# Up projection by Strassen's seven products, groups of 264 tokens, and a down stage that reads its input back from DRAM

## The chip, the cores and the metric

One core of one Trainium2 chip runs the whole kernel. The metric is the device time of one execution, in microseconds. The kernel before takes 1574.02 us (median of three runs, 1573.68 to 1574.51).

## What is computed

One layer over 1024 prompt tokens and 8 samples of 4 tokens (1056 tokens in all, 1024 features): a norm, a mixer (three kinds of recurrent heads between the products with `w_in` and `w_out`), a residual, and then the ConvFFN between two norms, with a second residual:

```
x  = x + rms_norm(mix, norm_mix_post)
hn = rms_norm(x, norm_ffn_pre)                      # x * rsqrt(mean(x * x)) * weight
up = einsum('bld,df->blf', hn, w_up)                # 1024 -> 2 * 2816
gate, val = up[..., :D_FF], up[..., D_FF:]
gate = causal_dwconv(gate, state, w, b)             # three taps along the tokens
out  = einsum('blf,fd->bld', gelu(gate) * val, w_down)   # 2816 -> 1024
x  = x + rms_norm(out, norm_ffn_post)
```

## The kernel before

Features lie on the 128 partitions, tokens along the row. The 1056 tokens are cut into `NG = 3` groups of `G = 352`. Every dense product works on a tile of 128 output features: `load_w` (L256 to L267) fetches a weight tile, ACT rounds it to `wh` (L264), POOL subtracts to get the remainder `wl` (L265), and the moving operand is held in the same way as `hh` and `hl`. `dense` (L269 to L278) then does three matmuls for each 128 features of the contraction: wh with hh, wh with hl, wl with hh. They are recorded under L203. Such a matmul has 352 columns.

The program is a sequence of parts:

- Mixer. The products with `w_in` fill the gaps of the recurrent chains; the order of the tensor engine is made by `Weave`, which places a step of a chain when a table `WAIT` of estimated times (ns) says its operands are there.
- Output projection, `project`, five tiles of `w_out` at first and the rest group by group; when a group has its sums of squares, `finish(g)` is woven in. It computes the norm's factor (`rstd_of`: a product with ones into a tile `po`, then Ln and Exp on ACT), and for each 128 features multiplies it in (L1629), adds the residual (L1630), writes the result to `x1_dram`, and splits it into `hh[g]` and `hl[g]` (`split_scaled`, L333) without waiting for the second norm. After `WAIT["f_rows"]` the factor of the second norm, `rs`, is made. From the end of this part on the tensor engine's order is no longer written by hand.
- ConvFFN. It goes through the 22 tiles of hidden features in five `QUARTERS`. For a tile, `gate_conv` multiplies a gate tile with all three groups (24 matmuls each), `scaled` (L303) multiplies the accumulated sums by `rs` on DVE on their way from PSUM to `fpre`, ACT does one tap (L212), DVE the other two (L1682), and ACT the gelu. `value` does the same product for the value tile, DVE multiplies (L303, L1695), ACT rounds to `hidh` (L1700), DVE subtracts to `hidl` (L1701). Both stay in SBUF until the down products of that quarter: 8 output tiles by 3 groups, added into `fa` by DVE (L1734).
- The last quarter's down products go group by group, so that the final norm and the output of a group run beside the products of the next.

In all the tensor engine does 7704 of these 352-column matmuls: 2376 with `w_in`, 576 with `w_out`, 3168 up, 1584 down. The lines below carry the up stage:

```
w = load_w(I["w_up"][2 * f], KD)                              # one 512 KB transfer, one cast, one subtraction
ps = drain(dense(accp, w, hn_operand, KD, g))                 # 24 matmuls
scaled(pre[:, 2 + g * G:2 + (g + 1) * G], ps, g, 0, G)
...
nc.scalar.copy(out=hidh[:, groups[g]], in_=hid)
vtt(out=hidl[:, groups[g]], in0=hid, in1=hidh[:, groups[g]].bitcast(F32), op=ALU.subtract)
```

Of the kernel before, what the change touches and what calls it, by code (L numbers as in the profile page):

```python
# [8 lines left out]
F32 = mybir.dt.float32  # L9
# [11 lines left out]
DS = 4  # L21
# [3 lines left out]
G = 352  # L25
NG = 3
# [5 lines left out]
QUARTERS = ((0, 5), (5, 10), (10, 14), (14, 18), (18, 22))  # L32
# [3 lines left out]
# (kind, unit, tiles as (section, tile in the section, conv tile or None))  # L36
# [6 lines left out]
# the order of the dense work of the mixer  # L43
# [3 lines left out]
# columns of the packed vectors  # L47
# [22 lines left out]
CUT = 4  # L70
# [23 lines left out]
def constants():  # L94
# [5 lines left out]
    # what takes the place of NEG and LV for the samples  # L100
# [92 lines left out]
def kernel(ctx: ExitStack, tc: tile.TileContext, I, O):  # L193
# [31 lines left out]
    hnp = ctx.enter_context(tc.tile_pool(name="hnp", bufs=1))  # L225
    wp = ctx.enter_context(tc.tile_pool(name="wp", bufs=2))
    left, right = ExitStack(), ExitStack()
# [22 lines left out]
    x1_dram = drp.tile([NG, P, KD, G], F32, name="x1_dram")  # L250
# [32 lines left out]
    def hn_operand(k, g):  # L283
        return hh[g][:, k, :], hl[g][:, k, :]
# [1596 lines left out]
```

## Time and profile before

| | |
|---|---|
| median of three runs | 1574.02 us |
| span of the profiled execution | 1578.6 us |
| busy: PE, DVE, ACT, POOL | 95%, 58%, 34%, 35% |
| mean granted clock of PE | 0.977 |
| bytes moved | 100.63 MB, 64 GB/s |

The profiled execution is 4.6 us above the median of the runs. A matmul's record stands for the time from its issue to its modelled end, so records overlap; the distance from one start to the next is what a matmul costs in a stream. PEld is the loading of weights, which runs beside PE. POOL is GpSimd, SP the engine that issues the transfers (its queue is SPq), and its instructions go out in order. In the records a granted clock of 1 is 2.4 GHz on the tensor engine, and stretches at half of that are 1.2 GHz.

### The profile page before, as it was taken

How to read it: one execution, taken by the hardware profiler on the slowest of the kernel's cores; microseconds unless marked ns; L12 is line 12 of the kernel's file. 1: busy time of each engine (PE TensorE's matmuls, PEld its weight loads, DVE VectorE, ACT ScalarE, POOL GpSimd, SP SyncE). 2: the span in 40 equal slices, each digit the busy share in tenths (PEclk: the TensorE clock that was granted, in tenths of full speed). 3: DMA queues.
4: the chain of work that ended last, by engine and by line, in shares of the span. 5: the costliest groups of instructions: out<-in, count | busy, mean ns of one | idle time of the engine just before them, and what ended most of it. 6: DMA issues, size and time to landing. Idle time of an engine off the chain costs nothing.

```text
span 1578.6 us, 24157 instructions
## 1 busy us (share of the span) xinstructions
PE 1496.2 (95%) x9438; PEld 1453.1 (92%) x9438; DVE 920.7 (58%) x1818; ACT 542.1 (34%) x1173; POOL 546.1 (35%) x624
## 2 busy tenths in 40 slices
PE   8788999989999999999899999999999999999995
PEld 8788899879989989988889999999999999999994
DVE  6889888796474367636975522444245325424558
ACT  7644445443342232424652211221122112212353
POOL 6234433232354353566432122221222222122224
PEclk9989999999999999999999999999999999999997
DMA  5111010111111231324531112111111111111142
GB/s 180 43 48 30 23 45 25 34 32 30 43 55 47 79 112 47 102 76 152 187 100 41 44 42 62 41 41 42 52 54 34 41 61 42 40 55 54 52 151 110
DMA packets 51210, 100.63 MB, mean 64 GB/s; under 512 B 14857, under 2 KB 25737, under 8 KB 50713
## 3 DMA queue, kind: packets, MB, share of 16 engines
q1 hardware_dynamic: 51096, 99.10, 20.1%
q8 instruction: 74, 1.21, 0.3%
q14 instruction: 40, 0.32, 0.1%
HBM read 85.25 MB, written 13.31 MB: 62 GB/s over the span
## 4 chain that ended last, share of the span: by engine, by line
PE 63%; DVE 17%; ACT 6%; POOL 5%; issue 4%; DMA 4%; SPq 0%; DVEq 0%; POOLq 0%; ACTq 0%
PE acc L203 55%; PE mc L203 3%; PE mb L203 3%; DVE kq L465 2%; PE mb L207 2%; DMA E<-rows_dram 2%; POOL wl L265 1%; DVE hl L333 1%; DVE two L784 1%; DVE v L465 1%; ACT sq L212 1%; POOL E L868 1%; PE po L203 1%; DVE fs L344 1%; ACT E L212 1%
## 5 line engine op out<-in xcount | busy, mean ns | idle before, releaser
L203 PE MATMUL acc<-hh,wh 128*128 128x352 f32 x1952 | 660.7, 339 | 18.2 <-DVE pre L303 12.2
L203 PE MATMUL acc<-hh,wl 128*128 128x352 f32 x1960 | 635.8, 324 | 2.6 <-POOL wl L265 2.0
L203 PE MATMUL acc<-hl,wh 128*128 128x352 f32 x1952 | 631.9, 324 | 0.7 <-DVE hl L333 0.7
L203 PEld LDWEIGHTS acc<-hh,wh 128*128 128x128 f32 x1952 | 371.7, 191 | 25.3 <-DVE pre L303 8.5
L265 POOL TENSOR_TENSOR wl<-w,wh 128x1024 fp32r<-128x1024 f32 (+2 forms) x117 | 252.9, 2162 | 362.3 <-ACT wh L264 354.8
L203 PEld LDWEIGHTS acc<-hh,wl 128*128 128x128 f32 x1960 | 372.4, 190 | 4.2 <-POOL wl L265 2.3
L203 PEld LDWEIGHTS acc<-hl,wh 128*128 128x128 f32 x1952 | 373.0, 191 | 3.1 <-DVE hl L333 1.7
L264 ACT CAST wh<-w 128x1024 fp32r<-128x1024 f32 (+2 forms) x117 | 109.9, 939 | 416.4 <-PE acc L203 400.3
L203 PE MATMUL acc<-hidh,wh 128*128 128x352 f32 x444 | 143.8, 324 | 0.0
L203 PE MATMUL acc<-hidh,wl 128*128 128x352 f32 x444 | 143.3, 323 | 0.0
L203 PE MATMUL acc<-hidl,wh 128*128 128x352 f32 x444 | 143.2, 322 | 0.0
L303 DVE TENSOR_TENSOR fpre<-acc,rs 128x352 f32<-128x352 f32 (+1 forms) x88 | 35.8, 430 | 137.5 <-PE acc L203 135.1
L1734 DVE TENSOR_TENSOR fa<-fa,acc 128x352 f32<-128x352 f32 x96 | 49.8, 519 | 106.3 <-PE acc L203 105.9
L1682 DVE SCALAR_TENSOR_TENSOR fy<-fpre,vec,fy 128x1072 f32<-128x1072 f32 x44 | 79.3, 1802 | 36.7 <-ACT fy L212 36.0
L203 PEld LDWEIGHTS acc<-hidh,wh 128*128 128x128 f32 x444 | 83.4, 188 | 0.0
L203 PEld LDWEIGHTS acc<-hidl,wh 128*128 128x128 f32 x444 | 83.4, 188 | 0.0
L203 PEld LDWEIGHTS acc<-hidh,wl 128*128 128x128 f32 x444 | 83.4, 188 | 0.0
L1701 DVE TENSOR_TENSOR hidl<-hid,hidh 128x352 fp32r<-128x352 f32 x66 | 52.7, 799 | 37.8 <-ACT hidh L1700 37.8
L1677 POOL COPY ffn_o<-fpre 128x2 f32<-128x2 f32 x22 | 4.1, 186 | 157.8 <-DVE fpre L303 157.8
L465 DVE SCALAR_TENSOR_TENSOR kq<-pre,cw,kq 128x352 f32<-128x352 f32 (+1 forms) x72 | 53.4, 748 | 7.7 <-ACT kq L212 7.2
L1700 ACT CAST hidh<-hid 128x352 fp32r<-128x352 f32 x66 | 31.9, 483 | 74.2 <-DVE hid L1695 49.9
L303 DVE TENSOR_TENSOR hid<-acc,rs 128x352 f32<-128x352 f32 x66 | 34.4, 521 | 38.1 <-PE acc L203 38.1
(552 smaller groups left out, 2238.7 us busy)
## 6 DMA issues: line engine op xcount, KB each, us to landing
w<-in_w_up_dram SPq DMA_DIRECT2D x44, 512.0 KB
w<-in_w_in_dram SPq DMA_DIRECT2D x30, 512.0 KB
E<-rows_dram SPq DMA_DIRECT2D x24, 256.0 KB
w<-in_w_dn_dram SPq DMA_DIRECT2D x21, 256.0 KB
w<-in_w_out_dram SPq DMA_DIRECT2D x10, 512.0 KB
w<-in_w_dn_dram SPq DMA_DIRECT2D x16, 320.0 KB
xr<-in_xT_dram SPq DMA_DIRECT2D x24, 176.0 KB
hh<-x_dram SPq DMA_DIRECT2D x3, 1408.0 KB
```

The source lines that it names most:

```text
L203: return nc.tensor.matmul(out, **kw)
L207: return nc.tensor.transpose(out, in_, identity)
L212: i = nc.scalar.activation(**kw)
L264: nc.scalar.copy(out=wh[:, ks], in_=w[:, ks])
L265: gtt(out=wl[:, ks], in0=w[:, ks], in1=wh[:, ks].bitcast(F32), op=ALU.subtract)
L303: vtt(out=out, in0=ps, in1=r, op=ALU.mult)
L333: stt(out=hl[g][:, k, :], in0=x, scalar=col(vcol + k), in1=hh[g][:, k, :].bitcast(F32), op0=ALU.mult, op1=ALU.subtract)
L465: stt(out=y[:, a:b], in0=pre[:, a + j:b + j], scalar=cw2[:, 4 * t + j:4 * t + j + 1], in1=y[:, a:b], op0=ALU.mult, op1=ALU.add)
L1682: stt(out=y[:, :LF], in0=pre[:, j:j + LF], scalar=col(V_FW + 3 * f + j), in1=y[:, :LF], op0=ALU.mult, op1=ALU.add)
L1700: nc.scalar.copy(out=hidh[:, groups[g]], in_=hid)
L1701: vtt(out=hidl[:, groups[g]], in0=hid, in1=hidh[:, groups[g]].bitcast(F32), op=ALU.subtract)
L1734: vtt(out=fa[:, g, m, :], in0=fa[:, g, m, :], in1=ps[:, :G], op=ALU.add)
```

## The change

The groups become four of 264 tokens everywhere, so all dense products now have 264 columns: 3168 matmuls with `w_in`, 768 with `w_out`, 2112 down.

The up product is made for pairs of output tiles, two halves of the contraction and pairs of token groups, that is as a 2 by 2 by 2 block product, with seven products instead of eight (Strassen's scheme in Winograd's form). `fast` does one pair of tiles for one or both pairs of groups (a unit `u`): seven products of 12 matmuls each, 168 matmuls for both units. Gate and value make 22 such calls, 3696 matmuls in all. The pair number 0 of the gate is made in two calls, one for each unit, with its weight pieces made twice.

`weight_pieces` fetches four pieces of 256 KB in a call, adds and subtracts them on DVE (four instructions of 128x512), and `weight_piece` rounds each of the seven to a high part on ACT and a remainder on POOL. `operands` makes the seven combinations of tokens once, in `finish`, on DVE and POOL (instructions of 128x1056), after the tokens were multiplied by the factor of the second norm (eight more instructions per group, L1649). `scaled` is gone from the FFN. The sums of products are put together on DVE as they come out of PSUM (`f6`, `f7`, `out`).

What the value side makes, `hid`, is written to `hid_dram` (22 transfers of 528 KB), read back in a down stage that begins after all up products (`hx`), and rounded and split there (ACT, DVE, 128x1056). The quarters are six. The tensor engine's order is written by hand to the end. The estimates in `WAIT` and the places of the norms of the input (`RSTD`) have other values.

```
-G = 352
-NG = 3
+G = 264
+NG = 4
-QUARTERS = ((0, 5), (5, 10), (10, 14), (14, 18), (18, 22))
+QUARTERS = ((0, 2), (2, 6), (6, 10), (10, 14), (14, 18), (18, 22))
-    s_norm=6310, rows1=9000, rows2=6960, rows3=8500, f_rows=18400, f_0=5120, f_1=8920,
+    s_norm=6310, rows1=9000, rows2=6960, rows3=8500, f_rows=14000, f_0=4000, f_1=5000, f_2=8000, f_last=3000,
-RSTD = [(1, 1), (1, 6), (2, 4)]
+RSTD = [(1, 1), (2, 1), (3, 1), (3, 6)]
+    hid_dram = drp.tile([NF, P, T], F32, name="hid_dram")
 def finish(g, wait=0):
...
-                split_scaled(m, k, V_FPRE, g)
                 square_sum(on, m, s2, k)
             yield WAIT["f_rows"]
-            if g == 1:
+            if g == NG - 2:
                 yield lambda: "projected" in have
-            rstd_of(new_rs(g), s2[:1])
+            r = rstd_of(on.tile([P, G], F32, name="rstd"), s2[:1])
+            for k in range(KD):
+                m = mix[k][:, groups[g]]
+                stt(out=m, in0=m, scalar=col(V_FPRE + k), in1=r, op0=ALU.mult, op1=ALU.mult)
+            operands(*divmod(g, 2))
+            have.add(("normed", g))
+        def operands(u, q):
...
+            t1, t2 = (on.tile([P, KH, G], F32, name=f"xt{i}") for i in range(2))
+            vtt(out=t1, in0=B[0][1], in1=B[0][0], op=ALU.subtract)
+            vtt(out=t2, in0=B[1][1], in1=t1, op=ALU.subtract)
+            split(6, t2)
+            split(5, t1, True)
+            vtt(out=B[0][1], in0=B[1][1], in1=B[0][1], op=ALU.subtract)
+            split(7, B[0][1])
+            gtt(out=t2, in0=B[1][0], in1=t2, op=ALU.subtract)
+            split(4, t2, True)
+            split(3, B[1][1])
+    QS = [(1, 0, 1), (6, 1, 0), (5, 2, 0), (7, 1, 0), (2, 0, 0), (4, 1, 0), (3, 2, 0)]
+        def weight_piece(x):
...
+            nc.scalar.copy(out=wh, in_=x)
+            gtt(out=wl, in0=x, in1=wh.bitcast(F32), op=ALU.subtract)
+        def weight_pieces(srcs):
...
+            for i, j in ((0, 0), (1, 0), (1, 1), (0, 1)):
+                A[i][j] = w[:, KH * i:KH * i + KH] if j == 0 else fg.tile([P, KH, P], F32, name="wq", bufs=2)
+                dma(out=A[i][j], in_=srcs[i][:, KH * j:KH * j + KH])
+            s1, s2 = (fg.tile([P, KH, P], F32, name=f"ws{i}") for i in range(2))
+            yield weight_piece(A[0][0])
+            vtt(out=s1, in0=A[1][0], in1=A[1][1], op=ALU.add)
+            vtt(out=s2, in0=s1, in1=A[0][0], op=ALU.subtract)
+            yield weight_piece(s2)
+            yield weight_piece(s1)
+            vtt(out=A[1][0], in0=A[0][0], in1=A[1][0], op=ALU.subtract)
+            yield weight_piece(A[1][0])
+            yield weight_piece(A[0][1])
+            yield weight_piece(A[1][1])
+            vtt(out=s2, in0=A[0][1], in1=s2, op=ALU.subtract)
+            yield weight_piece(s2)
+        def fast(srcs, units, out):
+            for (p, b, _), (wh, wl) in zip(QS, weight_pieces(srcs)):
+                for u in units:
...
+                    for k in range(KH):
+                        mm(ps, lhsT=wh[:, k, :], rhs=xh[:, k, :], start=first and k == 0, stop=False, **kw)
+                        mm(ps, lhsT=wh[:, k, :], rhs=xl[:, k, :], start=False, stop=False, **kw)
+                        mm(ps, lhsT=wl[:, k, :], rhs=xh[:, k, :], start=False, stop=k == KH - 1, **kw)
+                    if p == 1:
+                        nc.scalar.copy(out=sb[u, 1], in_=ps)
+                    elif p in (6, 7):
+                        vtt(out=sb[u, p], in0=sb[u, 1], in1=ps, op=ALU.add)
...
+                for j in range(2):
+                    dma(out=hid_dram[2 * i + j], in_=hids[j])
...
+            for f in range(f0, f1):
+                x = fp.tile([P, T], F32, name="hx", bufs=2)
+                dma(out=x, in_=hid_dram[f])
+                h, l = (fp.tile([P, T], F32R, name=f"hid{y}{f - f0}", bufs=2) for y in "hl")
+                nc.scalar.copy(out=h, in_=x)
+                vtt(out=l, in0=x, in1=h.bitcast(F32), op=ALU.subtract)
```

Three places of the order show what is moved. The first is DVE where the norms of the last token group end and the up products begin (`hl2`, `s20`, `mv` belong to `finish`, `fpre` to the gate; `ws` and `w` are weight pieces). Before:

```order
L333 SCALAR_TENSOR_TENSOR hl2_8179<-mkq_898,vec_75,hh2_8178 128x352 [waits Activation_49]
L1629 SCALAR_TENSOR_TENSOR mv_899<-mv_899,vec_75,rstd_8171 128x352
L341 TENSOR_TENSOR s20_8176<-s20_8176,s21_8177 128x352 [waits DVE_49,PE_49,Pool_49]
L1630 TENSOR_TENSOR mv_899<-mv_899,xr_8246 128x352 [waits DMAHW4_49,DVE_49]
L333 SCALAR_TENSOR_TENSOR hl2_8179<-mv_899,vec_75,hh2_8178 128x352 [waits Activation_49]
L344 TENSOR_TENSOR s20_8176<-s20_8176,sq1_8253 128x352 [waits Activation_49]
L303 TENSOR_TENSOR fpre_8288<-acc_8291,rs0_8079 128x352 [waits DMAHW5_49,DMAHW3_49,DMAHW6_49,DMAHW1_49,DMAHW7_49,DMAHW0_49,PE_49]
L303 TENSOR_TENSOR fpre_8288<-acc_8317,rs1_8166 128x352
```

After, at the same place, for the third of the four groups:

```order
L1649 SCALAR_TENSOR_TENSOR mix_1107<-mix_1107,vec_75,rstd_9571 128x264 [waits DMAHW6_49]
L1649 SCALAR_TENSOR_TENSOR mix_1107<-mix_1107,vec_75,rstd_9571 128x264 [waits DMAHW0_49]
L1649 SCALAR_TENSOR_TENSOR mix_1107<-mix_1107,vec_75,rstd_9571 128x264 [waits DMAHW3_49]
L1649 SCALAR_TENSOR_TENSOR mix_1107<-mix_1107,vec_75,rstd_9571 128x264 [waits DMAHW5_49]
L1649 SCALAR_TENSOR_TENSOR mix_1107<-mix_1107,vec_75,rstd_9571 128x264 [waits DMAHW7_49]
L1662 TENSOR_TENSOR hl6_9585<-mix_1107,hh6_9584 128x1056 [waits PE_49,Activation_49]
L1720 TENSOR_TENSOR ws1_9600<-ws0_9599,w_9592 128x512
L1723 TENSOR_TENSOR w_9592<-w_9592 128x512
L1727 TENSOR_TENSOR ws1_9600<-wq_9597,ws1_9600 128x512 [waits DMAHW2_49,Pool_49]
```

Before, the last DVE instructions of `finish` are followed by sums that leave PSUM, and no weight passes through DVE. After, the second weight piece that the first up product needs from DVE (`ws1_9600`) stands behind the eight norm multiplications of the group and a subtraction of 128x1056.

The second place is DVE in the middle of the up stage, before:

```order
L303 TENSOR_TENSOR fpre_8577<-acc_8632,rs2_8257 128x320 [waits PE_49]
L303 TENSOR_TENSOR fpre_8577<-acc_8632,rs2_8257 128x8x4
L1682 SCALAR_TENSOR_TENSOR fy_8661<-fpre_8577,vec_75,fy_8661 128x1072 [waits Activation_49]
L1682 SCALAR_TENSOR_TENSOR fy_8661<-fpre_8577,vec_75,fy_8661 128x1072 [waits DVE_49]
L303 TENSOR_TENSOR hid_8699<-acc_8674,rs0_8079 128x352 [waits PE_49]
L1695 TENSOR_TENSOR hid_8699<-fy_8467,hid_8699 128x352 [waits DVE_49]
L1701 TENSOR_TENSOR hidl1_8667<-hid_8699,hidh1_8666 128x352 [waits Activation_49]
L303 TENSOR_TENSOR hid_8729<-acc_8704,rs1_8166 128x352 [waits PE_49]
```

and after, from the end of a gate pair (L1784) into its value pair:

```order
L1784 TENSOR_TENSOR fpre_10732<-f6_10809,accr_10826 128x8x4
L1800 SCALAR_TENSOR_TENSOR fy_10967<-fpre_10732,vec_75,fy_10967 128x1072 [waits Activation_49]
L1800 SCALAR_TENSOR_TENSOR fy_10976<-fpre_10733,vec_75,fy_10976 128x1072 [waits Activation_49]
L1800 SCALAR_TENSOR_TENSOR fy_10967<-fpre_10732,vec_75,fy_10967 128x1072 [waits DVE_49]
L1800 SCALAR_TENSOR_TENSOR fy_10976<-fpre_10733,vec_75,fy_10976 128x1072 [waits DVE_49]
L1754 TENSOR_TENSOR f6_11043<-f1_11009,accr_11030 128x264 [waits PE_49,Activation_49]
L1754 TENSOR_TENSOR f6_11058<-f1_11024,accr_11045 128x264 [waits PE_49,Activation_49]
L1719 TENSOR_TENSOR ws0_11237<-w_11230,wq_11233 128x512 [waits DMAHW5_49,DMAHW4_49,Pool_49]
L1723 TENSOR_TENSOR w_11230<-w_11230 128x512 [waits DMAHW3_49,DVE_49,Pool_49]
L1754 TENSOR_TENSOR f7_11105<-f1_11009,accr_11030 128x264 [waits PE_49]
```

Before, the two taps (L1682) of one tile stand between sums of whole tiles. After, four taps (L1800) stand in a row ahead of `f6`, and the weight sums of the next call (L1719, L1723) stand ahead of `f7`, whose read of PSUM must be over before the sixth product of the same call adds to that bank.

The third is SP at the first down products, before:

```order
L263 DMA w_8959<-in_w_up_dram 128x1024 [waits DMAHW5_49,Pool_49]
L263 DMA w_9056<-in_w_up_dram 128x1024 [waits DMAHW6_49,Pool_49]
L263 DMA w_9155<-in_w_up_dram 128x1024 [waits DMAHW7_49,Pool_49]
L263 DMA w_9253<-in_w_dn_dram 128x640 [waits DMAHW1_49,DMAHW0_49,Pool_49]
L263 DMA w_9310<-in_w_dn_dram 128x640 [waits DMAHW1_49,Pool_49]
L263 DMA w_9367<-in_w_dn_dram 128x640 [waits DMAHW2_49,Pool_49]
```

and after:

```order
L1849 DMA out_ffn_dram<-ffn_o_9968 128x396 [waits Pool_49]
L1848 DMA hid_dram_88<-hid_14950 128x1056 [waits DVE_49]
L1900 DMA hx_15214<-hid_dram_88 128x1056 [waits DMAHW2_49,DMAHW1_49,DMAHW5_49,DMAHW0_49,DMAHW7_49,DVE_49,Pool_49]
L1848 DMA hid_dram_88<-hid_14949 128x1056 [waits DMAHW6_49,DVE_49]
L1900 DMA hx_15220<-hid_dram_88 128x1056
L268 DMA wd_15226<-in_w_dn_dram 128x256
L268 DMA wd_15264<-in_w_dn_dram 128x256
L268 DMA wd_15302<-in_w_dn_dram 128x256
```

Before, weights of the down products follow those of the up products and nothing else is fetched. After, the read of each of the first two hidden tiles (L1900) stands behind the last writes (L1848), and the first down weights behind these.

## Rows read from the trace of the kernel before

**Rows 1.** The page, busy time of engines: us, share of the span, instructions.
```profile
PE 1496.2 (95%) x9438; PEld 1453.1 (92%) x9438; DVE 920.7 (58%) x1818; ACT 542.1 (34%) x1173; POOL 546.1 (35%) x624
```

**Rows 2.** Stretches: length, busy (instructions) of PE, PEld, DVE, ACT, POOL; PE's clock.
```profile
0.00:747.50 747.50, 693.33 (x4490) 656.51 (x4490) 515.59 (x1205) 320.10 (x843) 325.46 (x421) 0.97 0.21 64
747.50:815.00 67.50, 58.06 (x311) 54.35 (x312) 59.69 (x91) 40.35 (x83) 28.57 (x19) 0.92 0.48 150
815.00:1509.00 694.00, 694.00 (x4343) 694.00 (x4343) 295.96 (x443) 149.43 (x188) 165.08 (x164) 1.00 0.16 51
1509.00:1578.60 69.60, 50.84 (x299) 48.24 (x297) 49.43 (x80) 32.22 (x61) 27.00 (x22) 0.87 0.30 113
```

**Rows 3.** The chain that ended last: start us, us, what.
```profile
748.30 1.21 DVE ss L344
758.27 3.16 DVE mix L1630 x2
783.84 2.65 DVE s L341
793.99 3.57 DMA w<-in_w_up_dram
814.71 694.66 PE acc L203 x4344
```

**Rows 4.** Matmuls of PE in turn, full clock: start us, us, operation.
```profile
899.83 0.32 PE L203 MATMUL acc<-hl,wh 128*128 128x352 f32 x1
...
902.37 0.32 PE L203 MATMUL acc<-hh,wl 128*128 128x352 f32 x1
```

**Rows 5.** The same where the granted clock is half.
```profile
796.55 0.50 PE L203 MATMUL acc<-hh,wh 128*128 128x352 f32 x1
...
798.89 0.50 PE L203 MATMUL acc<-hl,wh 128*128 128x352 f32 x1
```

**Rows 6.** Matmuls in plain float32, two records each, of 512 and 256 columns.
```profile
724.52 1.02 PE L203 MATMUL mb<-hh,hl 128*128 128x512 f32 x2
725.38 1.02 PE L203 MATMUL mb<-hl 128*128 128x512 f32 x2
```
```profile
189.79 1.89 PE L203 MATMUL mb<-kq 128*128 128x256 f32 x8
191.52 0.39 PE L203 MATMUL mc<-P,kw 128*128 128x128 f32 x2
```

**Rows 7.** DVE by line: busy us, mean ns; idle time before, and its releaser.
```profile
L1682 DVE SCALAR_TENSOR_TENSOR fy<-fpre,vec,fy 128x1072 f32<-128x1072 f32 x44 | 79.3, 1802 | 36.7 <-ACT fy L212 36.0
L1701 DVE TENSOR_TENSOR hidl<-hid,hidh 128x352 fp32r<-128x352 f32 x66 | 52.7, 799 | 37.8 <-ACT hidh L1700 37.8
L1734 DVE TENSOR_TENSOR fa<-fa,acc 128x352 f32<-128x352 f32 x96 | 49.8, 519 | 106.3 <-PE acc L203 105.9
```

**Rows 8.** Durations on DVE, ns: least, median, most.
```profile
L1682 DVE SCALAR_TENSOR_TENSOR fy<-fpre,vec,fy x44: 1331/1336/2400, 818.5 to 1491.1; 128x1072 f32<-128x1072 f32 x44
L1695 DVE TENSOR_TENSOR hid<-fy,hid x44: 524/525/1341, 823.8 to 1506.1; 128x352 f32<-128x352 f32 x44
L1699 DVE TENSOR_TENSOR hid<-fy,hid x22: 177/186/2389, 831.7 to 1511.4; 128x32 f32<-128x32 f32 x22
```

**Rows 9.** By line, DVE between 748 and 815 us.
```profile
L1630 DVE TENSOR_TENSOR mix<-mix,xr 128x352 f32<-128x352 f32 x15 | 11.8, 808 | 0.0
...
L1630 DVE TENSOR_TENSOR mkq<-mkq,xr 128x352 f32<-128x352 f32 x6 | 3.0, 511 | 0.0
...
L1629 DVE SCALAR_TENSOR_TENSOR mv<-mv,vec,rstd 128x352 f32<-128x352 f32 x3 | 1.7, 573 | 0.0
```

**Rows 10.** A weight transfer of 256 KB and the rounding around it: start us, us.
```profile
1498.86 1.29 POOL L265 TENSOR_TENSOR wl<-w,wh 128x512 fp32r<-128x512 f32 x1 [1.50 <-ACT wh L264]
1500.18 0.33 SPq L263 DMA_DIRECT2D w<-in_w_dn_dram  x1
1502.82 0.62 ACT L264 CAST fy<-w 128x512 fp32r<-128x512 f32 x1 [1.70 <-DMA w<-in_w_dn_dram]
```

More of the change, by code (lines that the diff above doesn't have):

```diff
@@ L1583, in project @@
                 w = load_w(I["w_out"][m], KD)
-                for g in range(2):
+                for g in range(NG - 1):
                     yield from product(m, w, g)
@@ L1603, in project @@
             ahead = KD - m
-            for g in range(2):
+            for g in range(NG - 1):
                 for n in range(KD - m):
@@ L1613, in project @@
                     load(n)
-                yield from product(ms[n], ws[n], 2)
+                yield from product(ms[n], ws[n], NG - 1)
                 if places[n:n + 1] == [None] and ahead < KD:
@@ L1703, with value_out, out @@
-        held, room, count = {}, [], [0] * NG
-        def down(qi, gs, fa, hid, ms=range(KD), between=None):
+        def value_out(ys, hids, fo):
+            def out(i, h, u, x, ps):
+                t0 = G * (2 * u + h)
+                if x is not None:
+                    t = fo.tile([P, G], F32, name="ft", bufs=3)
+                    vtt(out=t, in0=x, in1=ps, op=ALU.add)
+                    ps = t
+                for a, b, smp in quarter(u, h):
+                    if smp:
+                        o, p_ = (t.rearrange("p (b t) -> p b t", t=DS) for t in (hids[i][:, t0 + a:t0 + b], ps[:, a:b]))
+                        y = samp6(ys[i], SEQ + 2)[:, :, 0:DS]
+                    else:
+                        o, p_, y = hids[i][:, t0 + a:t0 + b], ps[:, a:b], ys[i][:, t0 + a:t0 + b]
+                    vtt(out=o, in0=y, in1=p_, op=ALU.mult)
+            return out
@@ new lines, in w_pair, with head @@
+        def w_pair(i, val):
+            return [I["w_up"][2 * (2 * i + j) + val] for j in range(2)]
+        pres = [gate_pre(f) for f in range(2)]
+        def head():
+            yield lambda: ("normed", 1) in have
+            yield from fast(w_pair(0, 0), (0,), gate_out(pres))
+            yield lambda: ("normed", NG - 1) in have
+            yield from fast(w_pair(0, 0), (1,), gate_out(pres))
+        weave.add(finish(NG - 1, WAIT["f_last"]), 8)
+        weave.add(head(), 9)
+        weave.run(lambda: not weave.streams)
@@ new lines @@
+        right.close()
+        with tc.tile_pool(name="fo", bufs=1, side="right") as fo:
+            ffn_o = fo.tile([P, NF, 18], F32, name="ffn_o")
+            st_ffn = fo.tile([P, NF, 16], F32, name="st_ffn")
+            dma(out=st_ffn, in_=I["st_ffn"])
+            for i in range(NF // 2):
+                if i:
+                    pres = [gate_pre(f) for f in range(2)]
+                    drain(fast(w_pair(i, 0), range(2), gate_out(pres)))
+                ys = [gate_conv(2 * i + j, pres[j], fo) for j in range(2)]
+                hids = [fo.tile([P, T], F32, name="hid", bufs=3) for j in range(2)]
+                drain(fast(w_pair(i, 1), range(2), value_out(ys, hids, fo)))
+                for j in range(2):
+                    dma(out=hid_dram[2 * i + j], in_=hids[j])
+            dma(out=O["ffn"], in_=ffn_o)
@@ new lines, with down, down_w @@
+    low.close()
+    with tc.tile_pool(name="fp", bufs=1) as fp, tc.tile_pool(name="accd", bufs=5, space=PSUM) as accd:
+        ssum = [sums(fp, f"fs{g}", 1) for g in range(NG)]
+        fa = fp.tile([P, NG, KD, G], F32, name="fa")
+        count = [0] * NG
+        def down(m, w, g, qi, hid):
+            nf = len(hid)
+            ps = drain(dense(accd, w, lambda k, g: [t[:, groups[g]] for t in hid[k]], nf, g))
+            if qi == 0:
+                nc.vector.tensor_copy(out=fa[:, g, m, :], in_=ps[:, :G])
+            else:
+                vtt(out=fa[:, g, m, :], in0=fa[:, g, m, :], in1=ps[:, :G], op=ALU.add)
+            if qi == len(QUARTERS) - 1:
+                if g == NG - 1 and count[g] == KD - 1:
+                    ssum[g].append(fp.tile([P, G], F32, name="sq1", bufs=2))
+                    act(out=ssum[g][1], in_=fa[:, g, m, :], func=AF.Square)
+                else:
+                    square_sum(fp, fa[:, g, m, :], ssum[g], count[g])
+                count[g] += 1
+        def down_w(qi, m, held=False):
```

263 lines of the change are left out of this document (133 added, 130 removed).

## The prediction

> **What bounds the kernel now.** I read the busy times first, then the stretches, the chain, and last the single rows. PE is busy 95% of the span and no other engine above 58% [rows 1], but that is a mean over four stages [rows 2]. Up to 747.5 us (mixer and most of the output projection) PE is busy 693 of 747.5 us. From 747.5 to 815 us (the norms of the three groups, with what is left of the projection and the first gate tile) it is busy 58 of 67.5, at a clock of 0.92, while DVE is busy 59.7. From 815 to 1509 us it is busy all of 694 us, at full clock. The last 70 us are the final norms. The chain says the same: one piece of 694.66 us with 4344 matmuls in a row, and ahead of it pieces of DVE and of a weight transfer [rows 3]. So in the third stage a change is worth what it does to the sum of matmul times, and anything that breaks the row of matmuls is added in full; in the second stage DVE sets the time.
>
> **The price of a matmul of 264 columns.** A 352-column matmul takes 160 ns: 4344 in 694.66 us, and 16 steps from 899.83 to 902.37 us [rows 3, 4]. At 2.4 GHz its columns alone are 146.7 ns, so 13.3 ns are on top. At half clock 8 steps take 2.34 us, 293 ns each, which is 352 columns at 1.2 GHz with nothing on top [rows 5]. No row has 264 columns. Plain float32 products, whose records take two clocks a column, show what kind of thing an excess is: 0.86 us for two of 512 columns is 430 ns (426.7 and 3), 1.73 us for eight of 256 is 216 ns (213.3 and 3) [rows 6]. There the excess is by the instruction and not by the column. Taking the 13.3 ns in the same way, 264 columns cost 110 + 13.3 = 123.3 ns. The ends: 112.7 ns if only the 2.7 ns of the float32 rows remain, and 130.7 ns if the moving columns and the 128 weight columns share one path ((352 + 128) / 160 ns is 3.0 columns a ns, and 392 / 3.0 is 130.7). In proportion it would be 120.0. I take 123.3.
>
> The Trainium skill (TensorE: Matmul & The Clock Gate, "Wait — 56ns, not 53.3ns?") says that a warm matmul costs its columns at 2.4 GHz and about 2.5 ns more, and that cold ones show no excess. The half-clock rows and the float32 rows agree; the 160 ns do not, since the rule would give 149.2 for 352 columns. By it 264 columns would cost 112.5 ns, close to the low end above.
>
> **The sum, stage by stage, against the span of 1578.6 us.**
>
> *First stage.* Up to the first norm of the projection, before issues 2775 of the 352-column matmuls, 444.0 us at 160 ns; after issues 3738 of 264 columns, 460.9 us at 123.3. The columns are the same within 1%, the instructions a third more. Some of the 17 us falls into the 54 us in which PE is idle there [rows 2]. Between 0 and +17 I take **+8**.
>
> *Second stage.* DVE sets it, so its instructions are counted. Before, from the first factor of the projection's norm to the first sum out of PSUM: 24 norm multiplications, 24 residuals, 24 subtractions of split_scaled, 16 sums. At the least disturbed means, 573 ns for the three-operand form and 511 for the other, these are 48.0 us; DVE is busy 59.7 [rows 2, 9]. So each takes 1.22 times its undisturbed time (808 against 511 for the same L1630, [rows 9]). After, the stretch that corresponds ends when pair 0's two gate calls are through. On DVE it holds four groups' work: up to the weight piece `ws1_9600` 48 three-operand forms, 41 others, 8 of 128x1056 and 2 of 128x512, and behind it 16, 24, 6 and 10 more. A DVE instruction costs 186 ns at 32 columns and 525 at 352 [rows 8], so 1.06 ns a column: 432 ns at 264, 695 at 512, 1271 at 1056, and 480 for the three-operand form. That is 52 us and then 33, 85 together, and with 1.22 it is 104. PE has 366 matmuls there, 45 us, which hide behind it. At least it lasts 85 us (no disturbance), at most 118 (DVE busy only 88% of it, as before); I take 100 against 67.5, **+32**. The order shows why PE cannot get ahead: the second weight piece stands behind the eight norm multiplications of the third group and a 128x1056 subtraction, its cast and its remainder behind casts and remainders of tokens.
>
> The Trainium skill (SBUF — State Buffer, "Who interferes with whom") says that a DVE instruction with two inputs in SBUF contends with a POOL instruction that reads SBUF, and one with a single SBUF input does not. The trace agrees: L1701 with both inputs in SBUF takes 799 ns on average, L1734 with one of them in PSUM 519 [rows 7]. It speaks against the change, whose weight sums and 128x1056 subtractions have both inputs in SBUF, beside more work on POOL.
>
> *Third stage, up.* Before: 3168 matmuls less 121 that are done by 815 us, 3047, 487 us. After: 3696 less 168, 3528, by 123.3 ns 435.0 us. To it come stalls inside the calls. In a gate call, the weights of the sixth piece can be rounded only when the third product has released their place. Cast 0.62, remainder 1.29, then the transfer into the freed `wq` 2.64 [rows 10], two weight sums of 0.69 that stand ahead of `f7` on DVE, and `f7` 0.43: 6.4 us and about 0.3 for the hand-overs (an estimate), while PE has four products of 12, 5.9 us. So 0.8 us in each of 10 calls. In a value call the four taps stand in a row ahead of `f6`; at 1.33 us undisturbed [rows 8] they are 5.3 us, at the mean of 1.80 [rows 7] 7.2, and begin only after two ACT operations on the whole row; I make the wait 1.2 us in each of 11 calls. Together 22 us; none if the transfers come earlier, 35 if the taps always take 1.8. I take 16. The stage: 451 − 487 = **−36**.
>
> *Down.* 1584 matmuls are 253.4 us, 2112 are 260.4: **+7**. At its start the last `hid` is written (528 KB), read back, rounded and split before a second tile of the quarter is there. Before, nothing stands there. 256 KB take 2.64 us [rows 10] and 512 KB 3.57 [rows 3], so write and read are some 7 us, and to them come a cast and a subtraction of 1.27; the products of the first tile cover little. Between 3 and 13, **+9**, part of it the half clock after the pause. What `hidh` and `hidl` cost on ACT and DVE before is hidden and goes for nothing.
>
> *End.* The last group is smaller by a quarter, and most of its norm's instructions with it: **−2**.
>
> The sum is 8 + 32 − 36 + 7 + 9 − 2 = +18, a span of 1597 us. The profiled execution lies 4.6 us above the median, so the time is **1592 us**, 1.1% slower. In matmul time alone the change saves 31 us (17 − 3 − 52 + 7); it is the second stage and the pauses that eat it.
>
> **Rivals.**
>
> *The excess is not there at 264 columns* (112.7 ns). For it: the float32 rows. Against: every 352-column row. First stage −11, second +28, up 3528 × 112.7 = 398 and, because the four products cover less, stalls of 26, 424 − 487 = −63; down −15 + 9, end −2: −54, a time of 1520. In proportion to the columns (120.0 ns) the same sum is 2 + 28 − 47 + 0 + 9 − 2 = −10, a time of 1564.
>
> *DVE is not disturbed and the pauses are hidden.* The second stage takes 85 us (+17), stalls in the calls 3 (up −49), the boundary 3, the first stage 3: 3 + 17 − 49 + 7 + 3 − 2 = −21, a time of 1553. For it: in the third stage DVE is busy only 296 of 694 us before [rows 2]. Against: the 1.22.
>
> *Everything in front of PE is late.* The second stage 118 us (+50), stalls 35 (−17), boundary 13, first stage +17, down +7, end −2: +68, a time of 1642. It decides when the taps stay at 1.8 us.
>
> *One path for weights and tokens* (130.7 ns): first stage +25, second +32, up 461 + 14 − 487 = −12, down 276 − 253 = +23, +9, −2: +75, a time of 1649. For it: 480 columns in 160 ns is a round 3.0. Against: half clock and float32 need no such path.
>
> **How the numbers follow.** Forecast 0.42 (its own range 1572 to 1612), no disturbance 0.18, no excess 0.12, proportion 0.08, all late 0.12, one path 0.08. About 0.2% is what a measurement can tell from no change. Faster are the second, third and fourth and a little of the first: 0.40; within 0.2% falls 0.06, mostly of the first; slower 0.54. The range from 1530 to 1632 leaves out most of the no-excess case and of the one-path case and part of all-late, about 0.2.
>
> **What would show it.** The start-to-start distance of two matmuls in the up stage: 123 ns, or 113, 120, 131. The length from the first `po` of the projection's norm to the end of pair 0's gate calls: 100 us, with DVE busy nearly all of it. In a gate call, a wait of PE before the sixth product, released by DVE `f7`; in a value call one before the fourth, released by `f6`. Between up and down a pause of some 9 us that ends with DVE's split of `hx`. I am wrong if the up stage comes out near 400 us or above 480, or if the second stage is under 85.

## The result and the profile after

The changed kernel takes 1648.1 us (median of four runs, 1644.9 to 1653.8), the kernel before 1574.3 beside it: a ratio of 1.0466, 95% interval 1.0439 to 1.0493. It is slower, as forecast, but by 4.7% instead of 1.1%, and outside the range.

The span of the profiled execution is 1645.4 us, 66.8 more. Its busy times, on the page:

```profile
PE 1465.7 (89%) x11486; PEld 1424.5 (87%) x11486; DVE 1060.3 (64%) x2247; ACT 623.6 (38%) x1425; POOL 695.4 (42%) x771
```

PE works 30.5 us less than before [rows 1]; the forecast had 31. So the whole loss is idle time. The stretches show where (columns as in [rows 2]); the cuts are the first product for the projection's norm, the end of pair 0's gate calls, the end of up, the begin of down:

```profile
0.00:782.30 782.30, 705.50 (x5455) 673.63 (x5455) 528.73 (x1344) 334.85 (x925) 322.50 (x426) 0.97 0.20 61
782.30:912.70 130.40, 63.70 (x384) 59.27 (x384) 105.26 (x153) 52.73 (x105) 67.10 (x48) 0.71 0.31 93
912.70:1355.80 443.10, 433.03 (x3530) 429.99 (x3528) 282.26 (x464) 153.66 (x253) 224.84 (x228) 1.00 0.21 75
1355.80:1366.40 10.60, 0.84 (x3) 0.53 (x3) 3.44 (x5) 3.06 (x5) 1.52 (x2) 0.73 0.81 257
1366.40:1645.40 279.00, 262.63 (x2120) 261.12 (x2120) 140.59 (x281) 79.32 (x137) 79.44 (x69) 0.96 0.33 108
```

| stage | before | forecast | after | forecast change | measured change |
|---|---|---|---|---|---|
| to the first norm product | 747.5 | 755.5 | 782.3 | +8 | +34.8 |
| norms and first gate | 67.5 | 100 | 130.4 | +32 | +62.9 |
| up | 487 | 451 | 443.1 | −36 | −43.9 |
| pause, down and end | 276.6 | 290.6 | 289.6 | +14 | +13.0 |

The two last rows came out within 8 us, both better than forecast. The two first are short by 27 and 31 us: they are the error, 66.8 us instead of 18.

The price of a matmul was near. From the chain of waits of the changed kernel (start us, us, what), one pair in the up stage and the first long piece of down:

```profile
1063.87 8.74 PE accr L206 x72
1072.62 2.93 PE acc L206 x24
1075.55 5.71 PE accr L206 x47
1081.33 0.64 ACT wh L1706 x2
1082.38 1.29 ACT fy L215
1083.69 4.65 DVE fy L1800 x3
1088.66 0.93 issue
1089.59 1.31 POOL wl L1707
1090.92 2.60 DMA wq<-in_w_up_dram
1093.64 0.70 DVE ws L1719
1094.42 1.60 DVE w L1723
1096.51 6.05 PE accr L206 x48
...
1366.37 226.81 PE acc L206 x1846
```

72 matmuls in 8.74 us are 121.4 ns each, 1846 in 226.81 are 122.9; 123.3 was taken. The first figure is as near to 120.0, the price in proportion to the columns, so these rows do not tell the two apart. The chain also has every member of the forecast stall: the cast, the taps, POOL's remainder, the transfer into the freed `wq`, two weight sums, and then products again. But the two kinds of stall are one: the taps delay the chain that ends at `f7`, once in each pair: ten of the twelve waits in the list below stand before the sixth product of a value call. The forecast had no link from the taps to that chain. POOL's timeline shows it: a memset of two columns of `fpre` waits for the taps, 3.8 us in each of ten pairs, and the remainder stands behind it. No run moved that memset.

```profile
1088.48 0.10 POOL L1793 MEMSET fpre<- 128x2 f32 x1 [3.77 <-DVE fy L1800]
1088.52 1.12 POOL L1794 COPY fpre<-st_ffn 128x16 f32<-128x16 f32 x1
1089.59 2.55 POOL L1707 TENSOR_TENSOR wl<-wq,wh 128x512 fp32r<-128x512 f32 x2
```

What the tensor engine waited for from 907 to 1355 us (us in total, times, longest):

```profile
PE accr L206 <- DVE f L1754: 10.0, 12, 1.7
PE accr L206 <- DVE fpre L1784: 1.0, 1, 1.0
PE accr L206 <- POOL wl L1707: 0.5, 1, 0.5
```

The pause between up and down, from the chain in that stretch:

```profile
1356.80 0.32 SPq L1848
1357.12 0.05 issue
1357.17 6.18 DMA hx<-hid_dram
1363.37 1.07 ACT hidh L1902
1364.44 0.31 ACT wdh L269
...
1364.89 1.44 POOL wdl L270
```

A write and a read are 6.2 us together, a cast 1.07; the last step is not DVE's split, as forecast, but the remainder of the first down weights on POOL, whose cast stood behind that of `hidh`. 10.6 us, forecast 9.

Second stage: the waits of the tensor engine, and of DVE, from 782.3 to 912.7 us:

```profile
PE accr L206 <- ACT wh L1706: 20.2, 1, 20.2
PE po L206 <- DVE s L354: 15.1, 3, 8.7
PE po L206 <- DVE ss L354: 10.4, 1, 10.4
PE accr L206 <- ACT hh L1661: 8.4, 1, 8.4
```
```profile
DVE ws L1727 <- POOL wl L1707: 3.5, 1, 3.5
DVE mix L1639 <- ACT rstd L322: 3.4, 2, 2.7
DVE ws L1720 <- POOL wl L1707: 3.0, 1, 3.0
DVE mix L1649 <- ACT rstd L322: 2.8, 2, 2.3
DVE f L1754 <- PE accr L206: 2.8, 2, 1.9
```

DVE is busy 105 us of the 130, and the forecast had 104. It is idle for 25 us in many small waits. The tensor engine is idle for 67 us, most of it for what DVE sets off. The longest wait, 20.2 us up to 856.8, is the one whose order the prediction named: between 830 and 850 us DVE is busy all the time, and the second weight piece (L1720) comes behind eight norm multiplications and a subtraction of 128x1056. DVE first, then ACT, which made the tensor engine wait:

```profile
849.28 5.06 DVE L1649 SCALAR_TENSOR_TENSOR mix<-mix,vec,rstd 128x264 f32<-128x264 f32 x7
854.26 1.24 DVE L1662 TENSOR_TENSOR hl<-mix,hh 128x1056 fp32r<-128x1056 f32 x1
855.43 0.68 DVE L1720 TENSOR_TENSOR ws<-ws,w 128x512 f32<-128x512 f32 x1
```
```profile
856.14 0.62 ACT L1706 CAST wh<-ws 128x512 fp32r<-128x512 f32 x1 [0.70 <-DVE ws L1720]
```

First stage: PE is busy 12.2 us more than before (693.3 and 705.5) and idle 22.6 us more (54.2 and 76.8). Its largest waits, before and after (first row of each answer):

```profile
PE acc L203 <- DVE pre L303: 12.2, 5, 4.4
```
```profile
PE acc L206 <- DVE pre L313: 27.5, 9, 9.6
```

### The profile page after: what moved, and what is told of

The parts are those of the page before. It is cut to its first block, busy times and chain, and to the rows that moved or that the text cites. A ratio compares the mean times of both kernels' runs of the same rounds, so it can differ in the third digit from the quotient of the medians.

```text
span 1645.4 us, 29719 instructions
## 1 busy us (share of the span) xinstructions
PE 1465.7 (89%) x11486; PEld 1424.5 (87%) x11486; DVE 1060.3 (64%) x2247; ACT 623.6 (38%) x1425; POOL 695.4 (42%) x771
## 5 line engine op out<-in xcount | busy, mean ns | idle before, releaser
L206 PE MATMUL acc<-hh,wh 128*128 128x264 f32 x1560 | 478.1, 307 | 35.0 <-DVE pre L313 27.5
L206 PE MATMUL acc<-hl,wh 128*128 128x264 f32 x1560 | 450.8, 289 | 0.8 <-DVE hl L344 0.7
L206 PE MATMUL acc<-hh,wl 128*128 128x264 f32 x1568 | 451.6, 288 | 0.0
L206 PE MATMUL accr<-hh,wh 128*128 128x264 f32 x880 | 255.0, 290 | 44.0 <-ACT wh L1706 20.2
L206 PE MATMUL accr<-hl,wh 128*128 128x264 f32 x880 | 252.9, 287 | 3.5 <-DVE hl L1662 3.5
L206 PE MATMUL accr<-hh,wl 128*128 128x264 f32 x880 | 252.7, 287 | 3.2 <-POOL wl L1707 3.2
L206 PEld LDWEIGHTS accr<-hh,wh 128*128 128x128 f32 x880 | 168.4, 191 | 48.1 <-ACT wh L1706 20.5
L206 PE MATMUL acc<-hidh,wdh 128*128 128x264 f32 x704 | 201.8, 287 | 9.0 <-ACT wdh L269 9.0
L206 PE MATMUL acc<-hidh,wdl 128*128 128x264 f32 x704 | 201.3, 286 | 0.8 <-POOL wdl L270 0.8
L206 PE MATMUL acc<-hidl,wdh 128*128 128x264 f32 x704 | 200.9, 285 | 0.0
```

The lines of the kernel that those rows point to most:

```text
L206: return nc.tensor.matmul(out, **kw)
```

## The experiments

Most variants were run once, with a profile; what is compared is a stage's length in the trace. "First product" is the start of the first product for the projection's norm (before 747.5, changed kernel 782.3; the variants of the changed kernel that leave the mixer alone have it between 781.4 and 788.3, so less than 7 us is no finding there; the variants of the kernel before are read beside runs of that kernel, too, and the seven beside e1_groups lay between 1576.4 and 1580.2). "Second stage" goes from there to the end of pair 0's gate calls (130.4; in four variants that are meant for the first stage, e4_first, e5_plan, e7_rstd and e11_plan_less, 127.4 to 131.4).

### The groups alone

**e1_groups**: the changed kernel up to `finish`, with the ConvFFN of before on groups of 264.

```
-            r = rstd_of(on.tile([P, G], F32, name="rstd"), s2[:1])
...
-            operands(*divmod(g, 2))
+            rstd_of(new_rs(g), s2[:1])
...
+                ps = drain(dense(accp, w, hn_operand, KD, g))
```

> The groups alone: the mixer and the projection of the changed kernel (four groups of 264), but the ConvFFN of the kernel before on groups of 264, with plain up products, the norm's factor multiplied in after the product, hid kept in SBUF and five quarters. 10272 matmuls of 264 columns. Theory A (the smaller groups themselves lengthen the mixer: a third more instructions and a shorter product per PSUM bank): the first product for the projection's norm starts at about 782 us as in the changed kernel, not at 747; the stage of the norms is about 68 us (64 three-operand forms and 52 others on DVE, 53 us undisturbed, times 1.22), and the span is about 782 + 68 + 497 (up) + 257 (down) + 23 = 1627 us. Theory B (the first stage is longer because of what Strassen's products want: their place in the planner's list, their buffers): the first stage returns to 747 to 760 us and the span to about 1595.

Measured 1647.5 us (four runs), ratio to before 1.0445, interval 1.0428 to 1.0463. Its stretches:

```profile
0.00:784.80 784.80, 704.91 (x5454) 673.49 (x5454) 533.29 (x1344) 335.34 (x925) 323.19 (x426) 0.97 0.20 60
784.80:858.80 74.00, 50.91 (x335) 46.58 (x334) 60.45 (x120) 43.33 (x105) 26.90 (x22) 0.86 0.46 141
858.80:1546.70 687.90, 687.87 (x5641) 687.87 (x5642) 297.79 (x537) 143.17 (x197) 156.25 (x158) 1.00 0.15 46
```

Theory A for the first stage: it is as long as in the changed kernel, so the groups make its delay, not Strassen's products. (The groups come with the changed kernel's `WAIT` and `RSTD` values; only `RSTD` was tried by itself, in e7_rstd.) For the span theory A had 1627 us, and it is 1643.0. More than that, the groups alone cost the whole 4.5%: of 64.4 us of span, 37.3 lie in the first stage, 6.5 in the second, and 20.6 behind it, where PE is busy 19.1 us more. The rest of the change, set on them, gains nothing: 528 matmuls fewer are 64 us, and some 50 us of them go into the second stage (130.4 us with 168 up products done by its end, against 74.0 with about 120), 10.6 into the pause and 10 into stalls.

### The first stage

**b3_twice** and **b2_split_all**, **b1_split** go the other way: they put the suspected costs into the kernel before.

```
# b3_twice
+            if k == ks[0] and weave.streams:
+                mm(ps[:, :G], lhsT=wh[:, k, :], rhs=xh, start=True, stop=True)
             mm(ps[:, :G], lhsT=wh[:, k, :], rhs=xh, start=(k == ks[0]), stop=False)
# b1_split, in conv_tile
+                for a, b in [(g * G, (g + 1) * G)] if g < 2 else [(704, 880), (880, 1080)]:
# b2_split_all, besides: in scaled and split_scaled
+        for c, d in [(0, n // 2), (n // 2, n)] if g == 2 and n > 300 else [(0, n)]:
+        for c, d in [(0, 176), (176, 352)] if g == 2 else [(0, G)]:
```

> The kernel before, three groups of 352 and all matmuls as they were, but in the convolution of the mixer the last group's part is worked off in two halves (880 and 1080 are the ends), so ACT and DVE have as many instructions there as with four groups: per tile one Identity, four three-operand forms and one Tanh more. Theory A (the first stage is longer because each group costs DVE its fixed part, 150 ns an instruction): DVE is 9 to 13 us busier before the first norm product, and that product starts at 760 to 770 us instead of 747.5. Theory B (the cause lies with the dense products, shorter ones in two PSUM banks and the order planned with them): it starts within 5 us of 747.5.

First product at 756.6 us, +9.1, between the two theories; DVE is 11.9 us busier, and the whole run took 1588.8 us against 1576.7 beside it.

```profile
0.00:756.60 756.60, 694.80 (x4489) 656.59 (x4489) 527.49 (x1277) 326.90 (x879) 322.27 (x420) 0.97 0.21 63
```

The tensor engine's order in the trace is that of the kernel before but for a few records. So DVE's instructions do cost time here, nearly what they take.

> As b1_split, and besides the sums that leave PSUM and the splits of the normed input are made in two halves for the last group, so that DVE and ACT have nearly all the instructions that four groups give them in the first stage, while the matmuls stay at 352 columns. b1_split started the first norm product at 756.6 us, 9 us late. Theory A (the instructions on DVE and ACT make the rest of the delay): 764 to 772 us. Theory B (the rest, some 14 us beyond 12 of matmul time and 9 of DVE, comes from the dense products themselves): 757 to 761 us.

757.5 us, +10.0 (1590.5 against 1580.7): theory B. The other instructions add no more than the scatter.

> The kernel before with the first matmul of each dense product of the mixer and of the projection made twice (its first result is overwritten): 114 matmuls of 352 columns more, 18.2 us at 160 ns, nothing else. Theory A (the tensor engine's time sets the first stage, so work added there is paid in full, and the 12 us that the smaller groups add in matmul time are too): the first norm product starts at 763 to 768 us instead of 747.5. Theory B (a good part falls into the 54 us in which the tensor engine is idle, as the prediction had it): 750 to 758 us.

772.0 us, +24.5 (1603.7 against 1580.7), for at most 18.2 us of matmuls.

```profile
0.00:772.00 772.00, 712.50 (x4596) 676.98 (x4597) 519.59 (x1206) 320.88 (x844) 322.81 (x421) 0.97 0.20 62
```

PE is busy 19.2 us more and idle 5.3 us more, so on balance nothing was absorbed in the idle time. But the edit does more than its expectation says ("nothing else"): the added matmuls go through the helper `mm`, which advances the planner's clock (`weave.now`) by 146.7 ns for each, and the trace shows chain steps and dense products in another order from about 115 us on. What the matmuls cost alone, in the order of before, was not measured.

> The kernel before with both edits that lengthened its first stage: the first matmul of each dense product twice (b3_twice, +24.5 us, though 17 to 18 us of matmuls were added) and the last group's work on DVE and ACT in halves (b2_split_all, +10.0 us). Theory A (these two, matmul time that is paid in full and more, and the fixed part of the instructions on DVE, are what the smaller groups cost): 778 to 786 us for the first norm product, where the changed kernel has 782. Theory B (they overlap, and something else is missing): 772 to 776 us.

769.2 us, +21.8, neither: the two do not add up, and even together they leave 13 of the 34.8 us. The tensor engine's order is nearly that of b3_twice, and set on it DVE's added instructions cost nothing.

**e4_first** sets the instructions that empty PSUM early in DVE's order, **e7_rstd** the factors of the input norm early in the tensor engine's.

```
+        with tc.high_priority(offset=FIRST):
+            vtt(out=out, in0=ps, in1=r, op=ALU.mult)
```

> The changed kernel, but every multiplication that takes a dense product out of PSUM stands as early in DVE's order as the chains' steps. Theory A (a product of 264 columns gives DVE 2.9 us instead of 3.8 to empty one of two banks, and DVE comes late because chain work stands ahead): the tensor engine's waits for `pre` fall from 27.5 us to under 15, and the first norm product starts at 772 us or earlier. Theory B (the waits are for the factors of the input norm and for the chains themselves): the waits stay over 22 us and the product at 778 to 790 us.

The waits for `pre` fell from 27.5 to 16.9 us, less than theory A wanted, but the first product came at 779.6, 2.7 us earlier, within the scatter: as much waiting came back elsewhere. The largest wait of a list was not the price of the stage.

```
-RSTD = [(1, 1), (2, 1), (3, 1), (3, 6)]
+RSTD = [(1, 1), (1, 6), (2, 4), (3, 4)]
```

> The changed kernel with the factors of the input norm made earlier in the tensor engine's order: at the same places as before for the first three groups and right behind for the fourth. Theory A (the 9.6 us wait at 83 us and its like come from accumulators that cannot be emptied until a factor is there): the waits for `pre` fall by 8 us or more and the first norm product starts at 775 us or earlier. Theory B (not the factors): 780 to 788 us.

782.1 us, waits for `pre` 29.3: theory B.

**e5_plan**, **e11_plan_less**, **b5_plan** change only what the planner reckons for a matmul of these products.

```
-        weave.now += max(n, 64) * (1 if r.dtype == F32R else 4) / 2.4
+        weave.now += max(n, 64) * (1 if r.dtype == F32R else 4) / 2.4 + (12 if r.dtype == F32R else 0)
# e11_plan_less: - (10 ...); b5_plan, in the kernel before: + (13.3 ...)
```

> The changed kernel, but the planner that places the chains' steps between the dense products reckons 122 ns for a matmul of 264 columns, which is measured, where it reckoned 110. Theory A (the first stage's extra 22.6 us of idle time come from a plan that thinks the dense products shorter than they are, so chain steps stand too late or too early): idle time of the tensor engine before 782 us falls from 76.8 us to 60 or less and the first norm product starts at 765 us or earlier. Theory B (the cause is work on DVE between dense products, whatever the plan): the first norm product stays at 775 to 790 us.

> The changed kernel with a planner that reckons 100 ns for a matmul of 264 columns (110 in the changed kernel, 122 in e5_plan, where the first norm product came at 792.4 us). Theory A (the order that the plan makes moves the first stage by ten microseconds either way, and the part of the delay that matmul time and DVE's instructions leave open is such a shift): the first norm product comes 5 us or more away from 782 us. Theory B (the plan hardly matters): within 4 us of 782.

> The kernel before with a planner that reckons 160 ns for a matmul of 352 columns, which is measured, where it reckoned 146.7. Theory A (the plan's order is worth ten microseconds in either kernel, and that of the kernel before lies well): the first norm product comes at 752 us or later instead of 747.5. Theory B (a plan nearer to the measured times is better or the same): 740 to 750 us.

792.4, 779.6 and 765.1 us. In the changed kernel the truer estimate costs 10 us (more than either theory of e5_plan, and 4 beyond the latest of the variants above), and the less true one changes nothing beyond the scatter (theory B there). In the kernel before, the measured price instead of one too low by 13.3 ns costs 17.6 us, with the same instructions (1599.4 us against 1573.2 beside it for the whole run; single runs of the kernel before lie between 1573 and 1582). The first product of that run:

```profile
765.10 0.86 PE L203 MATMUL po<-ss,ones 128*128 128x352 f32 x2 [0.21 <-DVE ss L344]
```

So the order in which chain steps and dense products stand can be worth 17.6 us by itself, more than the instructions that were put on DVE. How much of b3_twice's 24.5 us is its own new order stays open. Of the two orders of the kernel before that differ by the estimate alone, its own is the better one; no others were tried.

### The second stage

**e3_po_first** and **e2_one_call** move unit 0's products behind the norms. Their expectations count the stage to 907.0 us (124.7) instead of 912.7 (130.4), so what is compared with them is the difference.

```
# e3_po_first
-            yield lambda: ("normed", 1) in have
+            yield lambda: ("normed", 1) in have and ("first", NG - 1) in have
# e2_one_call
-            yield from fast(w_pair(0, 0), (0,), gate_out(pres))
             yield lambda: ("normed", NG - 1) in have
-            yield from fast(w_pair(0, 0), (1,), gate_out(pres))
+            yield from fast(w_pair(0, 0), range(2), gate_out(pres))
```

> The changed kernel, but unit 0's products of pair 0 are recorded only after the product for the last group's first norm, so that product no longer stands behind them on the tensor engine; the product for its second norm still does, and weight pieces are still made twice. Theory A (the wait of that one product): the stage is some 10 to 14 us shorter, about 112 us. Theory B (amount of work on DVE): within 3 us of 124.7 us.

The product for the last group's first norm came 13.7 us sooner (68.0 us behind the first product instead of 81.7), as theory A wanted, but the stage was 129.6 us: theory B.

> The changed kernel, but the up products begin only when all four groups have their norms, and pair 0's gate is one call for both units, so its weight pieces are made once. Theory A (in the second stage the tensor engine's order holds the last group's first norm product behind the second up product of unit 0, which waits for weights, so DVE is left without work): the stage from the first norm product to the end of pair 0's gate calls falls from 124.7 us to about 110: 14 us for the wait, some 4 for the weight pieces, and less than 8 back because unit 0's 84 products (10.2 us) no longer lie in the gaps. Theory B (the amount of work on DVE alone sets the stage, 104 us busy): the stage loses only the 3.5 us of the doubled weight sums and gains the 10 us of unit 0's products, so it is 125 to 132 us.

124.9 us, 5.5 less, where theory A wanted some 15 less and theory B 0 to 7 more: neither, and not far outside the scatter. From there to the first down product it took 475 us instead of 452, with 21 us of waits for `f` instead of 10, and PE was busy 445 us instead of 433 for the same number of matmuls, at a mean granted clock of 0.96 instead of 1.00. Why the waits doubled was not pursued.

**e9_no_norm**, **e10_no_sums**, **e6_no_pool** change the amount of work.

```
# e9_no_norm: seven of a group's eight multiplications left out
+                if k == 0:
                     stt(out=m, in0=m, scalar=col(V_FPRE + k), in1=r, op0=ALU.mult, op1=ALU.mult)
# e10_no_sums: operands from plain blocks
-            vtt(out=t1, in0=B[0][1], in1=B[0][0], op=ALU.subtract)
...
+            split(6, B[1][1])
# e6_no_pool
-                (gtt if on_pool else vtt)(out=lo, in0=x, in1=hi.bitcast(F32), op=ALU.subtract)
+                vtt(out=lo, in0=x, in1=hi.bitcast(F32), op=ALU.subtract)
```

> The changed kernel without seven of the eight multiplications of a group's tokens by the second norm's factor (their result is left out): 28 instructions fewer on DVE in the second stage, 17 us at their 0.6 us. Theory A (DVE's amount of work sets the stage, wherever it lies): the 130 us from the first norm product to the end of pair 0's gate become 110 to 115. Theory B (a chain that goes over several engines sets it, in which only the last groups' multiplications lie): 119 to 125.

```profile
781.70:897.00 115.30, 62.99 (x384) 58.95 (x384) 94.98 (x125) 52.15 (x105) 68.11 (x48) 0.78 0.34 106
```

115.3 us, 15.1 less for 28 instructions of some 0.6 us: at the edge of theory A. DVE is busy 10.3 us less and idle 4.8 us less (20.3 instead of 25.1), so its work counts at least one for one.

> The changed kernel without the sums of token blocks (the operands are plain blocks, rounded and split as before): six 128x1056 instructions fewer on DVE, two fewer on POOL in the second stage, 7.6 us undisturbed on DVE. Theory A (amount of work on DVE): 120 to 123 us for the stage. Theory B (chain: t1, t2, their casts and the POOL sum follow one another after the last norm, about 10 us with POOL's 3.4): 115 to 120.

120.5 us, 9.9 less for six instructions on DVE and two on POOL. It lies half a microsecond from theory B, which is less than the scatter: the run shows that the sums count, not which of the two theories holds.

> The changed kernel, but all sums and remainders of the token operands are made on DVE, none on POOL (seven instructions of 128x1056 more on DVE, 8.9 us undisturbed, and as many fewer on POOL). Theory A (DVE is slowed by POOL's use of SBUF in the second stage, and POOL's own 3 us instructions lie on the chain): the 130 us from the first norm product to the end of pair 0's gate become 122 or less. Theory B (DVE's amount of work sets the stage): they become 137 to 142.

```profile
788.30:910.90 122.60, 62.14 (x384) 58.57 (x384) 101.41 (x161) 53.36 (x105) 45.13 (x38) 0.74 0.31 99
```

122.6 us, theory A at its edge. Eight more instructions on DVE (the expectation says seven; the trace has 161 instead of 153) made DVE's busy time shorter (105.3 to 101.4 us), with POOL busy 22 us less. DVE's long instructions show where it went, in the changed kernel and in this run (by line, 784 to 912 us):

```profile
L1662 DVE TENSOR_TENSOR hl<-mix,hh 128x1056 fp32r<-128x1056 f32 x6 | 9.7, 1617 | 0.0
L1674 DVE TENSOR_TENSOR mix<-mix 128x1056 f32<-128x1056 f32 x2 | 4.8, 2382 | 0.0
```
```profile
L1662 DVE TENSOR_TENSOR hl<-mix,hh 128x1056 fp32r<-128x1056 f32 x8 | 9.9, 1249 | 0.0
L1674 DVE TENSOR_TENSOR mix<-mix 128x1056 f32<-128x1056 f32 x2 | 2.5, 1250 | 0.0
```

The Trainium skill (SBUF — State Buffer, "Who interferes with whom") has that DVE with two inputs in SBUF contends with POOL's reads; this run agrees. The span gained only 2.2 us (1643.2), since the first product came at 788.3.

**e8_warm** puts products that nothing reads ahead of the second and third products of pair 0's two gate calls.

```
+                    if p in (6, 5) and len(units) == 1:
+                        idle = accr.tile([P, 512], F32, name="accr")
+                        for _ in range(30):
+                            nc.tensor.matmul(idle[:, :P], lhsT=ones, rhs=ones, start=True, stop=True)
```

> The changed kernel with 30 float32 products of 128 columns that nothing reads ahead of the second and third products of pair 0's gate calls (120 in all, 13 us at the full clock, 26 at half), where the tensor engine waits for weights. Theory A (the granted clock of 0.70 in the second stage costs what its matmuls take longer, 60 us against 45): the 130 us from the first norm product to the end of pair 0's gate become 122 to 126. Theory B (the chain over DVE, ACT and POOL sets the stage, the clock does not matter): 129 to 134.

143 us, outside both. The mean clock rose from 0.71 to 0.79, but PE was busy 25.6 us more, and the stage is 12.6 us longer; what the clock costs here stays open.

## Why the prediction was wrong

Right, by its own steps: the matmul of 264 columns (123.3 forecast, 121.4 to 122.9 measured; 112.7 and 130.7 fall; 120.0 does not, so whether the excess goes by the instruction is open, but with 120.0 the same sum is 1564 us and fails in the same two stages), PE's total saving (31 and 30.5), up (−36 and −43.9: stalls of 10 instead of 16, and 122.7 ns a matmul in the mean of the stage), the pause (9 and 10.6), down and end. The mechanism of the second stage was right as well: DVE sets it, with the busy time that was worked out (its factor, 59.7 over 48.0, is 1.24 and not 1.22, which would have made 106 us).

Two terms were mis-sized.

*First stage, "Some of the 17 us falls into the 54 us in which PE is idle".* This step failed: +8 was taken, and it is +34.8. A busy share of 93% was read as room. In the changed kernel PE is busy 12.2 us more, and its idle time did not shrink but grew by 22.6. The step also priced DVE's extra instructions at nothing, and they are 10 us (b1_split, b2_split_all), and it did not ask what another order of chain steps and products costs: the estimate alone is worth 17.6 us (b5_plan). These two effects are shown, each alone, in the kernel before. That matmuls put in beside the chains are not absorbed is shown only together with a new order (b3_twice: at most 18.2 us put in, 24.5 us out). How the 34.8 us divide in the changed kernel is open, since the effects do not add (b4_both).

*Second stage, "I take 100".* The work on DVE was put at 104 us, and 100 was taken, as if DVE could never wait and some of its work lay outside. It was busy 81% of the stage, not even the 88% that made the upper end of 118. With four groups, each with two norms, there are eight hand-overs DVE to PE (`po`), ACT (`rstd`) and back, and the weight pieces go DVE, ACT, POOL, DVE. That the place of unit 0's products in the tensor engine's order was to blame fell (e3_po_first); the amount of work on DVE, at one for one or more, and POOL beside it hold (e9_no_norm, e10_no_sums, e6_no_pool). What holds DVE's 20 to 25 idle us in place is not shown by a run.

Of the rivals, "one path for weights and tokens" gave 1649, nearly the time that came, and that is luck: the 121 ns refute it. "Everything in front of PE is late" gave 1642 and is nearest in mechanism, but its sum comes out in part by chance, too: it had stalls of 35 in the up stage where 10 came, a first stage of +17 where 35 came, and a second stage of +50 where 63 came.

## What to carry to other kernels

Idle time of the bounding engine in a stage that is woven from chains was no room for more work here: price added work there in full, and the planned order as a cost of its own when durations change. Where a stage is set by a busy engine through hand-overs, its length is not the busy time; even the busy time divided by the share that the engine reached before was too little here (105 / 0.88 = 119 us, where 130 came). And where a change has a side that applies to the whole program (here the group size), price that side by itself first: alone it cost as much as the whole change.

## What the runs showed that was not expected

The order of chain steps and products can be worth more than work added to an engine: a change of 13.3 ns in an estimate, with no instruction added, moved the first stage of the kernel before by 17.6 us. And DVE did more instructions in less time when POOL's share was given to it: 101.4 us for 161 instructions against 105.3 for 153. And a memset of two columns on POOL, standing ahead of a weight remainder, ties the weights to DVE's taps: POOL idles 3.8 us before it in each of ten pairs, and ten of the twelve waits in the up stage come behind it.
